# A two-layer encoder on one core: two pairs of heads in one score burst, the Exp table loaded early, one maximum per head, halves at the end, PSUM banks for turned blocks, and a new table of places

## The chip, the cores and the metric

The kernel runs on one core of one Trainium2 chip. The metric is device time in microseconds (us) of one execution. TensorE (PE; its weight loads are shown as PEld), VectorE (DVE), ScalarE (ACT), GpSimd (POOL) and SyncE (SP) each run their own instruction stream in order; DMA transfers are issued by SP, by POOL and, at the start, by ACT.

## The reference, cut to what matters

Two layers over 256 tokens of width 1024, everything in float32. A layer is an attention part with three groups of heads and a feed-forward part with a convolution:

```python
h = rms_norm(x, n1);  proj = h @ w_in            # 1024 -> 2560
# a: 4 heads, neighbourhood with a bias; d: 6 heads, dilated window; c: 6 query heads on 2 key heads
s = q @ k.T * scale (+ bias);  p = softmax(s);  out = p @ v
x = x + concat(rms_norm(out_a), rms_norm(out_d), rms_norm(out_c)) @ w_out
h = rms_norm(x, n2);  g, u = split(h @ w_gate_up)   # 1024 -> 2 x 2816
g = depthwise_conv_centred(g, cw, cb)               # 3 taps along the tokens
x = x + (gelu(g) * u) @ w_down
```

## The kernel before, in words

Tokens are two tiles of 128 partitions (t = 0, 1). Each product is made of three: a float32 operand is split into a rounded high part and a low rest, and `mm3` (line 695) multiplies high by high, high by low and low by high. A weight unit of up to 2048 columns comes by DMA into one of four `raw` buffers; ACT copies it to `hi` in chunks and DVE subtracts to make `lo` (`split`, line 666). `hi` and `lo` have two buffers each. During the feed-forward part of layer 0, six units of layer 1's output projection are split ahead and stored to DRAM (`keep`, line 624); layer 1 fetches them with DMAs that POOL issues into `hi` and `lo`.

**Start.** `load(0)` (line 640) issues the first loads by the list START: on ACT's queue the first two column blocks of x, on SP's queue the gains of the first norm (tile `gl0`, 8 KB), the identity, the four chunks of the first weight unit and the other six blocks of x, between each other. Then come the units 1 and 2 and the rest. x is turned block by block (`split_T`, line 708): two PE transposes (one for each t) give a block of 256 tokens; ACT scales it by its gain into `hT` (high), DVE makes the low part. Two blocks share one PSUM bank, and the planner below treats a bank as one thing. `warmed` (line 578) issues dummy bf16 matmuls, first 13, then 15 that fill gaps.

**Layers.** The projections (seven groups of columns, 12 units) accumulate in four PSUM banks (`psa`). The attention works in the other four banks (`psw`): for every pair of heads a burst of 12 score matmuls (`scores`, line 1210; two heads on the two halves of the rows, run side by side), then softmax (`softens`, line 1062: DVE's maximum, ACT's Exp with the sum, a reciprocal, a scaling), four transposes of the result (`turn`), and the product with the values (`weigh`). Projections and output projections are woven between. The heads of group c, which have no bias, take their maximum with one `reduce_max` for each t. The output projection of group a comes last (line 1305), each half of columns after the sums of squares of the group: `group_rstd` turns them (two transposes of `sqm`), DVE sums, POOL takes the root (`rstd`), and DVE adds to x (tile `xs`, named `const_x` in the profile). Then x is turned again for the second norm. The feed-forward part has 11 steps: gate (two PSUM tiles, the convolution on ACT and DVE, Gelu), up, and down, which accumulates four tiles of 128 x 512 (`dacc`). After the last step DVE adds each of the four to x, and in layer 1 SP stores each to the output (line 1443).

**What sets the order.** Everything is recorded first as a list of operations (`Plan`, line 238) and then put in order by a list scheduler (`order`, line 319): it takes the operation that could start first by its own table of costs (`cost`, line 473), and among those that could start at the same time the one of lowest rank. The rank is the place in the list, plus what `later` adds, plus an entry of the table PLACES (line 229) for this place. The tuple LANDS (line 52) gives the landing of each first load by its number in START; the landing of later DMAs is worked out from a rate. The engines then run their instructions in the order that came out, each waiting for its semaphores. SP's DMAs also wait in turn for eight semaphores, so the ninth DMA is issued only after the first has landed, and so on.

Of the kernel before, what the change touches and what calls it, by code (L numbers as in the profile page):

```python
# [11 lines left out]
F32 = mybir.dt.float32  # L12
# [38 lines left out]

LANDS = (4074, 3054, 5167, 3987, 5363, 6065, 7002, 7704, 8406, 9342, 10278, 10308, 10337)

# [171 lines left out]
def handover(a, b):  # L225
# [3 lines left out]
PLACES = {  # L229
# [5 lines left out]
}  # L235


class Plan:
    def __init__(self, tc):
        self.tc, self.ops, self.shift, self.burst, self.bursts, self.behind = tc, [], 0, None, {}, None  # L240
        for name, short in (("tensor", "PE"), ("scalar", "ACT"), ("vector", "DVE"), ("gpsimd", "POOL"), ("sync", "SP")):
            setattr(self, name, PlanEngine(self, short, getattr(tc.nc, name)))
# [26 lines left out]
    def add(self, engine, method, args, kw):  # L269
# [14 lines left out]
        if method == "matmul" and not kw["start"]:  # L284
            ins.append(args[0])
        o.ns, o.lat, o.size, o.kind = cost(engine.name, method, args, kw, ins)
        o.before, o.after, o.first, o.tiles = set(), [], [], []
        for v in ins + outs:
# [30 lines left out]
    def order(self):  # L319
# [79 lines left out]
        while len(done) < len(ops):  # L399
            best = None  # L400
            for e, r in ready.items():
                for i in r:
                    o = ops[i]
                    if e in opened:
                        if o.burst != opened[e]:
                            continue
                        at = at_of(o)
                    elif o.burst is not None:
                        at = at_of_burst(o.burst) if i == self.bursts[o.burst][0] else None
                    else:  # L410
                        at = at_of(o)
                    if at is not None and (best is None or (at, o.rank) < best[:2]):
                        best = (at, o.rank, i)
# [22 lines left out]
            if o.method == "dma_start":  # L436

                ring = e if i < self.first_loads else "SP"
                end = max(at + 1360, wires.get(ring, 0.0))
                shared = 0.0  # L440
                if i < self.first_loads:
                    shared = o.size if ring == "ACT" else min(o.size, 120 * max(0.0, wires.get("ACT", 0.0) - end))
                if e == "POOL":
                    end += 1000
                wires[ring] = end + shared / 120 + (o.size - shared) / (280 if i < self.first_loads else 335)
                end = wires[ring] + 1200
                if i < self.first_loads:
                    end = LANDS[sum(p.method == "dma_start" for p in ops[:i])]
# [24 lines left out]
def cost(engine, method, args, kw, ins):  # L473

    out = args[0]
    if method == "dma_start":
        w = out if isinstance(out, View) else args[1]
        small = min(out.shape[-1], args[1].shape[-1]) < 128
        spread = isinstance(args[1], bass.AP) and args[1].ap[0][0] == 0
        size = 4 * math.prod(w.shape) * (2 if small else 2 if spread else 1)  # L480
        return 620 if engine == "POOL" else 480, 0, size, None
# [33 lines left out]
def encoder_kernel(  # L515
# [73 lines left out]
    minus_half = const.tile([P, 32], F32, tag="mh", name="minus_half")  # L589
    nc.gpsimd.memset(minus_half, -0.5)  # L590


# [115 lines left out]
    def split_T(srcs, hi, lo, k0, g, name):  # L708
# [3 lines left out]
        for b in range(0, n, 2):  # L712
            m = min(2, n - b)
            ps = psw.tile([P, 2, S], F32, tag="w", name=f"pt_{name}_{b}")
            for i in range(m):
                k = b + i
                for t in range(NT):
                    nc.tensor.transpose(
                        ps[:, i, t * P : (t + 1) * P], srcs[t][:, k * P : (k + 1) * P], ident
                    )  # L720
            for i in range(m):
                k = b + i
                h, o = hi[:, k0 + k], lo[:, k0 + k]
                nc.scalar.activation(h, ps[:, i], AF.Copy, scale=g[:, k : k + 1])
                nc.vector.scalar_tensor_tensor(
                    o, ps[:, i], g[:, k : k + 1], h.bitcast(F32), ALU.mult, ALU.subtract
                )
# [147 lines left out]
    for l in range(DEPTH):  # L875
# [181 lines left out]
        class Head:  # L1057
# [3 lines left out]

            def softens(self, sps):

# [141 lines left out]
        def na_bias(h):  # L1205

            flat = nabs[l].rearrange("p r c -> p (r c)")
            return [flat[:, (h * RPB_ROWS + 3 - 2 * t) * GRID_W :][:, :S] for t in range(NT)]

        def scores(i):  # L1210

            two = heads[i : i + 2]
            sps = [psw.tile([P, NT, S], F32, tag="w", name=f"s_{z.name}") for z in two]
            g = two[0].group
            with nc.together():
                for t in range(NT):
                    for x, y in ((0, 0), (0, 1), (1, 0)):
                        for z, sp, rows_ in zip(two, sps, (LOW, HIGH)):
                            nc.tensor.matmul(
                                sp[:, t], turned[g + "q"][x][rows_, z.h // 2, t * P : (t + 1) * P],  # L1220
                                turned[g + "k"][y][rows_, z.kv if g == "c" else z.h // 2],
                                start=(x, y) == (0, 0), stop=(x, y) == (1, 0),
                            )
            for z, sp in zip(two, sps):
                z.softens([sp[:, t] for t in range(NT)])

# [146 lines left out]
        def gate(s):  # L1373
# [15 lines left out]
            nc.scalar.activation(B, A, AF.Gelu)  # L1389
            made[s] = B  # L1390

        def up(s):
# [9 lines left out]
        def down(steps):  # L1402
            ws = [unit() for _ in steps]
            for h in range(2):
                hs = slice(h * 512, (h + 1) * 512)
                for t in range(NT):
                    c = slice(t * P, (t + 1) * P)
                    for s, (wh, wl) in zip(steps, ws):
                        ch, cl = ready[s]
                        for j in range(2):  # L1410
                            mm3(
                                dacc[t][h], ch[:, j, c], cl[:, j, c], wh[:, j, hs], wl[:, j, hs],
                                s == 0 and j == 0, s == STEPS - 1 and j == 1,
                            )

# [21 lines left out]
        for h in range(2):  # L1437
            for t in range(NT):
# [3 lines left out]
                )  # L1442
                if l == DEPTH - 1:
                    nc.sync.dma_start(ov[:, t, hs], xs[:, t, hs])
    nc.emit()
# [69 lines left out]
```

## Time and profile before

| | us |
|---|---|
| median of 3 runs (614.57 to 614.73) | 614.73 |
| the profiled execution | 614.38 |
| its span, first to last instruction | 612.6 |
| PE busy in the span | 604.5 |
| DVE busy | 485.4 |
| ACT busy | 428.5 |
| POOL busy | 84.3 |

The difference of 1.8 us between the execution and its span lies ahead of the first and behind the last instruction. All of the kernel is emitted by one line (L470), so instructions are told apart by the tiles that they write and read: `psw_w<-const_ident,const_x` is a transpose of x, `psa_a<-wp_hi,act_hT` a projection, `psw_w<-act_ko,act_qo` a score matmul. The layers stand one after the other: attention of layer 0 up to about 113 us, its feed-forward part to about 308, attention of layer 1 to about 420, its feed-forward part to the end. A busy PE is not PE at its peak: a matmul's row lasts longer than the distance to the next matmul's start, so PE's pace is read from starts.

### The profile page before, as it was taken

The numbers are of one execution on the slowest core, as the hardware profiler recorded it, in microseconds if no ns is written. First come the engines' busy times: TensorE is split into PE (matmuls) and PEld (weight loads), VectorE is DVE, ScalarE is ACT, GpSimd is POOL, SyncE is SP. The second block draws the span as 40 slices with busy tenths as digits, with TensorE's granted clock in tenths as the row PEclk, the third lists the DMA queues.
The fourth block names the chain that finished last, engine by engine and source line by source line (L and its number), as shares of the span: only waits on it lengthen the run. The fifth ranks groups of instructions, "written<-read, shape, count | busy, mean of one in ns | idle before, by whom it ended". The sixth has DMA issues, their size and how long they took to land.

```text
span 612.6 us, 9883 instructions
## 1 busy us (share of the span) xinstructions
PE 604.5 (99%) x3484; PEld 525.2 (86%) x3484; DVE 485.4 (79%) x1000; ACT 428.5 (70%) x1064; POOL 84.3 (14%) x136
## 2 busy tenths in 40 slices
PE   8999999999999999999999999998999999999997
PEld 6998888888888888888899989887888888888885
DVE  4899989797788988887777788767877777777774
ACT  6789999696565766675588889857755656566661
POOL 2732130202400000000032214231000000000000
PEclk9999999999999999999999999999999999999999
DMA  8893403557589799987555626654665555556501
GB/s 272 294 294 141 139 25 105 184 159 242 166 225 326 247 360 326 349 293 251 155 155 182 215 70 240 206 178 129 202 217 179 175 197 201 167 185 205 189 18 68
DMA packets 85073, 121.44 MB, mean 198 GB/s; under 512 B 9864, under 2 KB 69608, under 8 KB 85024
## 3 DMA queue, kind: packets, MB, share of 16 engines
q1 hardware_dynamic: 82752, 112.17, 56.6%
q0 software_dynamic: 1728, 8.39, 4.0%
q8 instruction: 27, 0.44, 0.3%
q10 hardware_dynamic: 544, 0.26, 0.2%
q14 instruction: 22, 0.18, 0.1%
HBM read 110.93 MB, written 9.88 MB: 197 GB/s over the span
## 4 chain that ended last, share of the span: by engine, by line
PE 92%; DVE 2%; ACT 2%; POOL 1%; DMA 1%; issue 1%; SPq 0%; DVEq 0%; POOLq 0%
PE psw_w L470 51%; PE psa_a L470 41%; DMA const_x<-in_x_dram 1%; ACT act_s2k L470 1%; POOL small_rstd L470 1%; DVE const_x L470 1%; DVE wp_lo L470 1%; SPq L470 0%; DVE act_sw L470 0%; DVE act_z L470 0%; ACT wp_hi L470 0%; POOL small_ms L470 0%; ACT L470 0%; ACT act_z L470 0%; ACT act_hT L470 0%
## 5 line engine op out<-in xcount | busy, mean ns | idle before, releaser
L470 DVE TENSOR_TENSOR wp_lo<-wp_raw,wp_hi 128x512 fp32r<-128x512 f32 (+2 forms) x332 | 232.1, 735 | 53.9 <-ACT wp_hi L470 36.8
L470 ACT CAST wp_hi<-wp_raw 128x512 fp32r<-128x512 f32 (+2 forms) x332 | 202.5, 663 | 21.7 <-PE psa_a L470 9.1
L470 PE MATMUL psw_w<-act_hT,wp_hi 128*128 128x512 f32 x704 | 181.4, 393 | 0.0
L470 PEld LDWEIGHTS psw_w<-act_hT,wp_hi 128*128 128x128 f32 x704 | 128.1, 189 | 24.7
L470 PE MATMUL psa_a<-wp_hi,act_hT 128*128 128x384 f32 (+2 forms) x448 | 113.3, 332 | 0.5 <-ACT wp_hi L470 0.5
L470 PEld LDWEIGHTS psw_w<-act_hT,wp_lo 128*128 128x128 f32 x704 | 97.9, 190 | 6.9
L470 PE MATMUL psw_w<-act_hT,wp_lo 128*128 128x256 f32 x704 | 102.8, 282 | 0.0
L470 PEld LDWEIGHTS psa_a<-wp_hi,act_hT 128*128 128x128 f32 x448 | 78.1, 189 | 4.0 <-ACT wp_hi L470 0.8
L470 PE MATMUL psa_a<-wp_lo,act_hT 128*128 128x384 f32 (+2 forms) x224 | 74.2, 333 | 0.3 <-DVE wp_lo L470 0.2
L470 ACT COPY act_s2k<-psw_w 128x256 f32<-128x256 f32 x88 | 32.2, 371 | 58.7 <-PE psw_w L470 58.5
L470 PE MATMUL psa_a<-wp_lo,act_ch 128*128 128x512 f32 x176 | 69.4, 394 | 0.0
L470 PE MATMUL psa_a<-wp_hi,act_cl 128*128 128x512 f32 x176 | 69.4, 395 | 0.0
L470 PE MATMUL psa_a<-wp_hi,act_ch 128*128 128x512 f32 x176 | 68.9, 394 | 0.0
L470 DVE TENSOR_TENSOR act_s2k<-psw_w,act_s2k 128x256 f32<-128x256 f32 x88 | 36.7, 422 | 15.2 <-ACT act_s2k L470 14.9
L470 PEld LDWEIGHTS psa_a<-wp_lo,act_hT 128*128 128x128 f32 x224 | 42.2, 188 | 3.0 <-DVE wp_lo L470 1.7
L470 PEld LDWEIGHTS psa_a<-wp_hi,act_cl 128*128 128x128 f32 x176 | 33.2, 188 | 7.9 <-DVE act_cl L470 0.3
L470 PEld LDWEIGHTS psa_a<-wp_hi,act_ch 128*128 128x128 f32 x176 | 33.2, 189 | 6.7
L470 PEld LDWEIGHTS psa_a<-wp_lo,act_ch 128*128 128x128 f32 x176 | 33.1, 188 | 6.8
L470 DVE SCALAR_TENSOR_TENSOR act_s2k<-act_s2k,act_cw,act_s2k 128x255 f32<-128x255 f32 x88 | 36.8, 482 | 1.4 <-ACT act_s2k L470 1.3
L470 ACT ACTIVATE act_s2k<-act_s2k,act_cw 128x256 f32<-128x256 f32 x44 | 24.1, 595 | 18.0 <-DVE act_s2k L470 18.0
L470 ACT ACTIVATE act_s2k<-act_s2k 128x512 f32<-128x512 f32 x22 | 13.9, 631 | 30.0 <-DVE act_s2k L470 30.0
L470 POOL TENSOR_TENSOR small_rstd<-small_ms,const_mh 128x6 f32<-128x6 f32 (+2 forms) x26 | 31.7, 1218 | 2.2
(112 smaller groups left out, 794.7 us busy)
## 6 DMA issues: line engine op xcount, KB each, us to landing
wp_raw<-in_w_gate_up_dram SPq DMA_DIRECT2D x44, 1024.0 KB, 5.2
wp_raw<-in_w_down_dram SPq DMA_DIRECT2D x22, 1024.0 KB, 5.0
wp_raw<-in_w_in_dram SPq DMA_DIRECT2D x14, 768.0 KB, 6.3
wp_raw<-in_w_in_dram SPq DMA_DIRECT2D x8, 1024.0 KB, 8.8
wp_raw<-in_w_out_dram SPq DMA_DIRECT2D x8, 768.0 KB, 9.5
dram_khi<-act_mixT_hi SPq DMA_DIRECT2D x4, 768.0 KB, 9.5
dram_klo<-act_mixT_lo SPq DMA_DIRECT2D x4, 768.0 KB, 9.8
wp_lo<-dram_klo POOLq DMA_DIRECT2D x4, 768.0 KB, 5.4
```

The source lines that it names most:

```text
L470: getattr(o.engine.real, o.method)(*map(real, o.args), **{k: real(v) for k, v in o.kw.items()})
```

## The change

- `scores`: 16 bursts of one pair become 10. BURSTS says where two pairs (24 matmuls, four PSUM banks) go as one: heads d0 to d3, c0 to c3 and a0 to a3 in each layer.
- After the last Gelu of layer 0 ACT computes one Exp of a 128 x 1 constant, which loads the table of Exp there.
- `softens`: one `reduce_max` over both t for a head of group c.
- `split_T`: each turned block has a PSUM bank of its own.
- `down` of the last two steps in layer 1: the tile (t, h) = (1, 1) is computed as two tiles of 256 columns, the second in a bank of psw (`end`); DVE's addition and the store of this tile are split in the same way, 512 to 768 and 768 to 1024.
- The planner: other LANDS, other rates for DMAs (360 for 335 GB/s, 1000 for 1200 ns to land, no extra 1000 ns for POOL's), 1.5 times the size for stores to DRAM, 1290 ns for a change of table, ties broken by place; and a new PLACES with 69 entries for 49. Some stand at the first loads: 35 (`gl0`), 40 (x, blocks 2 and 3), and 89 to 91 (units 1 and 2).

```diff
-LANDS = (4074, 3054, 5167, 3987, 5363, 6065, 7002, 7704, 8406, 9342, 10278, 10308, 10337)
+LANDS = (4100, 3300, 5300, 3450, 5800, 6450, 7250, 8200, 8900, 9800, 10700, 10750, 10800)
 PLACES = {
-    715: 185, 722: 185, 772: -261, 980: -22, 982: -95, 983: -95, 1039: -192, 1146: -2, 1150: -159, 1350: 23,
+    35: 21, 40: 129, 59: -58, 60: -58, 61: -58, 75: -24, 89: -285, 90: -285, 91: -285, 497: 135, 499: 135, 500: 135,
...
+    3994: -106, 4040: 30, 4120: 17, 4169: -28, 4188: -44, 5572: 165,
 }
...
-                if e == "POOL":
-                    end += 1000
-                wires[ring] = end + shared / 120 + (o.size - shared) / (280 if i < self.first_loads else 335)
-                end = wires[ring] + 1200
+                wires[ring] = end + shared / 120 + (o.size - shared) / (280 if i < self.first_loads else 360)
+                end = wires[ring] + 1000
                 if i < self.first_loads:
                     end = LANDS[sum(p.method == "dma_start" for p in ops[:i])]
...
-            ps = psw.tile([P, 2, S], F32, tag="w", name=f"pt_{name}_{b}")
+            ps = [psw.tile([P, S], F32, tag="w", name=f"pt_{name}_{b + i}") for i in range(m)]
...
-                    for t in range(NT):
-                        nc.vector.reduce_max(nm[:, t : t + 1], sps[t], axis=AX.X, negate=True)
+                    nc.vector.reduce_max(nm, whole, axis=AX.X, negate=True)
...
+        BURSTS = {0: 2, 4: 1, 6: 2, 10: 1, 12: 2}
+        scored = {}
+
         def scores(i):
 
-            two = heads[i : i + 2]
-            sps = [psw.tile([P, NT, S], F32, tag="w", name=f"s_{z.name}") for z in two]
-            g = two[0].group
-            with nc.together():
-                for t in range(NT):
...
+            if i in BURSTS:
+                with nc.together():
+                    for n in range(i, i + 2 * BURSTS[i], 2):
+                        two = heads[n : n + 2]
+                        sps = [psw.tile([P, NT, S], F32, tag="w", name=f"s_{z.name}") for z in two]
+                        scored[n] = sps
...
             nc.scalar.activation(B, A, AF.Gelu)
             made[s] = B
+            if s == STEPS - 1 and l + 1 < DEPTH:
+                with nc.not_before("ACT"):
+                    nc.scalar.activation(few_out, minus_half[:, :1], AF.Exp)
...
+                    halved = l == DEPTH - 1 and steps[-1] == STEPS - 1 and (h, t) == (1, 1)
+                    if halved:
+                        end = psw.tile([P, S], F32, tag="w", name="end")
+                    for a, b in ((512, 768), (768, 1024)) if halved else ((hs.start, hs.stop),):
...
+        if l == DEPTH - 1:
+            hs = slice(768, 1024)
+            nc.vector.scalar_tensor_tensor(xs[:, 1, hs], hold["end"], r2[:, 1:2], xs[:, 1, hs], ALU.mult, ALU.add)
+            nc.sync.dma_start(ov[:, 1, hs], xs[:, 1, hs])
```

The first place where rows move is SP's queue at the start of the program; `act_s2k<-in_norm` is `gl0`, `wp_raw<-in_w_in` with 128x384 a chunk of the first unit, with 128x2x384 a half of unit 1, with 128x4x384 a whole unit (2, then 3). Before:

```order
L470 DMA act_s2k_81<-in_norm_g_dram 16x128
L470 DMA const_ident_89<-in_c_ident_dram 128x128
L470 DMA wp_raw_95<-in_w_in_dram 128x384 x2
L470 DMA const_x_79<-in_x_dram 128x2x256
L470 DMA wp_raw_95<-in_w_in_dram 128x384 x2
L470 DMA const_x_79<-in_x_dram 128x2x256 x2
L470 DMA act_s2k_131<-in_out_norm_g_dram 16x128
L470 DMA act_s2k_131<-in_norm_g_dram 16x128
L470 DMA wp_raw_141<-in_w_in_dram 128x2x384 x2
L470 DMA wp_raw_155<-in_w_in_dram 128x4x384
```

The same queue in the changed kernel, from its first DMA on:

```order
L473 DMA const_ident_81<-in_c_ident_dram 128x128
L473 DMA wp_raw_89<-in_w_in_dram 128x384
L473 DMA wp_raw_95<-in_w_in_dram 128x2x384 x2
L473 DMA wp_raw_105<-in_w_in_dram 128x4x384
L473 DMA wp_raw_89<-in_w_in_dram 128x384 x3
L473 DMA const_x_79<-in_x_dram 128x2x256 x2
L473 DMA act_s2k_129<-in_norm_g_dram 16x128
L473 DMA act_s2k_138<-in_out_norm_g_dram 16x128
L473 DMA act_s2k_138<-in_norm_g_dram 16x128
L473 DMA wp_raw_156<-in_w_in_dram 128x4x384
L473 DMA const_rot_163<-in_c_rot_dram 128x2x208
L473 DMA const_x_79<-in_x_dram 128x2x256
```

Units 1 and 2 moved ahead of three chunks of unit 0 and of all x on this queue; `gl0` went from first to behind them, and one load of x, which by its number is blocks 2 and 3, to behind unit 3 and `rot`.

The second place is PE at the end of layer 1's attention, where group a's output projection (`psa_a<-wp_..,act_mixT`), the transposes of `sqm` and those of x for the second norm meet. Before, from the transposes of `sqm` on:

```order
L470 MATMUL psw_w_162<-const_ident_89,act_sqm_1010 128x128 x2
L470 MATMUL psw_w_122<-const_ident_89,act_s2k_221 128x88
L470 MATMUL psa_a_153<-wp_hi_136,act_mixT_lo_886 128x512
L470 MATMUL psa_a_159<-wp_hi_136,act_mixT_hi_870 128x512
L470 MATMUL psa_a_159<-wp_lo_248,act_mixT_hi_870 128x512
L470 MATMUL psa_a_159<-wp_hi_136,act_mixT_lo_886 128x512
L470 MATMUL psw_w_120<-const_ident_89,const_x_79 128x128
```

In the changed kernel ten matmuls of the same unit stand behind the transposes of `sqm`, and these are the last rows of them and what follows; `wp_hi_167` and `wp_lo_180` are the parts of the next unit, the second half of columns:

```order
L473 MATMUL psa_a_169<-wp_hi_142,act_mixT_hi_889 128x512
L473 MATMUL psa_a_169<-wp_lo_151,act_mixT_hi_889 128x512
L473 MATMUL psa_a_169<-wp_hi_142,act_mixT_lo_904 128x512
L473 MATMUL psa_a_161<-wp_hi_142,act_mixT_lo_904 128x512
L473 MATMUL psa_a_297<-wp_hi_167,act_mixT_hi_889 128x512
L473 MATMUL psa_a_327<-wp_hi_167,act_mixT_hi_889 128x512
L473 MATMUL psw_w_133<-const_ident_81,const_x_79 128x128 x2
```

Four matmuls between the transposes of `sqm` and those of x became twelve, and two of the twelve read the next unit. That unit is fetched by POOL, whose queue is there, in the changed kernel:

```order
L473 TENSOR_TENSOR act_sqm_972<-act_sqm_972,act_sqm_893 128x256
L473 DMA wp_hi_167<-dram_khi_2861 128x1024
L473 DMA wp_lo_180<-dram_klo_2881 128x1024
L473 TENSOR_SCALAR small_ms_351<-small_ss_1412 128x2
L473 TENSOR_TENSOR small_rstd_357<-small_ms_351,const_mh_85 128x2
```

Before, the two DMAs of that unit stood ahead of the addition to `sqm`, with `wp_lo` first.

The third place is the end of PE's program in the changed kernel; `psw_w_83` is the tile `end`, `psa_a_169` the tile (t, h) = (0, 0) of the down product, and before the last rows were six of the tile (1, 1), 512 wide:

```order
L473 MATMUL psw_w_83<-wp_hi_142,act_ch_821 128x256
L473 MATMUL psw_w_83<-wp_lo_151,act_ch_821 128x256
L473 MATMUL psw_w_83<-wp_hi_142,act_cl_831 128x256
L473 MATMUL psa_a_169<-wp_lo_151,act_ch_821 128x512
L473 MATMUL psa_a_169<-wp_hi_142,act_cl_831 128x512
L473 MATMUL psa_a_169<-wp_hi_142,act_ch_821 128x512
L473 MATMUL psa_a_169<-wp_lo_151,act_ch_821 128x512
L473 MATMUL psa_a_169<-wp_hi_142,act_cl_831 128x512
```

The entry 5572 put the last five matmuls of tile (0, 0) behind the halves of tile (1, 1), so a tile of 512 columns is finished last again.

More of the change, by code (lines that the diff above doesn't have):

```diff
@@ L239, in __init__ @@
     def __init__(self, tc):
-        self.tc, self.ops, self.shift, self.burst, self.bursts, self.behind = tc, [], 0, None, {}, None
+        self.tc, self.ops, self.shift, self.burst, self.bursts, self.behind, self.table = tc, [], 0, None, {}, None, AF.Exp
         for name, short in (("tensor", "PE"), ("scalar", "ACT"), ("vector", "DVE"), ("gpsimd", "POOL"), ("sync", "SP")):
@@ L411, in order @@
                         at = at_of(o)
[L412 removed]
+                    if at is not None and (best is None or (at, o.rank, i) < best):
                         best = (at, o.rank, i)
@@ L479, in cost @@
         spread = isinstance(args[1], bass.AP) and args[1].ap[0][0] == 0
-        size = 4 * math.prod(w.shape) * (2 if small else 2 if spread else 1)
+        stored = isinstance(out, View) and out.tile.pool.dram
+        size = 4 * math.prod(w.shape) * (2 if small or spread else 1.5 if stored else 1)
         return 620 if engine == "POOL" else 480, 0, size, None
```

57 lines of the change are left out of this document (35 added, 22 removed), and 9 rows, old and new, of the table PLACES.

## The prediction

> **What bounds the kernel now.** I read the page first, for the busy shares, then PE's waits, then the start stretch by stretch, since that is where the change moves most. Page:
>
> ```profile
> PE 604.5 (99%) x3484; PEld 525.2 (86%) x3484; DVE 485.4 (79%) x1000; ACT 428.5 (70%) x1064; POOL 84.3 (14%) x136
> ```
>
> PE's waits (us in total, times, longest):
>
> ```profile
> PE psw_w L470 <- DVE const_x L470: 1.6, 2, 1.3
> PE psw_w L470 <- POOL const_warm L470: 1.0, 1, 1.0
> PE psw_w L470 <- ACT act_s2k L470: 0.5, 1, 0.5
> ```
>
> PE is busy 604.5 of 612.6 us, and its three largest waits together are 3.1 us. So the time is PE's program plus a few holes. Two things can move it: instructions that PE no longer spends (or spends anew), and holes that open or close. DVE and ACT count only where PE waits for them. There is little to win and any amount to lose.
>
> **The start: the largest term.** Windows of the first 20 us (the columns after the stretch are its length, busy time of PE, PEld, DVE, ACT and POOL, granted clock, DMA share and GB/s):
>
> ```profile
> 0.00:4.00 4.00, 3.02 (x15) 2.15 (x16) 0.00 (x0) 1.28 (x1) 2.73 (x10) 1.00 0.48 116
> 4.00:10.00 6.00, 5.95 (x35) 4.49 (x33) 3.44 (x8) 4.17 (x11) 0.00 (x0) 1.00 0.92 277
> 10.00:14.00 4.00, 3.50 (x23) 2.88 (x23) 2.56 (x8) 3.76 (x13) 0.34 (x2) 1.00 1.05 388
> 14.00:20.00 6.00, 6.00 (x33) 5.70 (x34) 4.32 (x9) 5.94 (x33) 2.82 (x5) 1.00 1.07 360
> ```
>
> The DMA engines are nearly full from 4 us on (share 0.92 and more), so a load arrives when the bytes issued ahead of it have gone. The DMA issues of the same stretch (KB each, median us from issue to landing):
>
> ```profile
> wp_raw<-in_w_in_dram SPq DMA_DIRECT2D x5, 768.0 KB, 9.2
> wp_raw<-in_w_in_dram SPq DMA_DIRECT2D x4, 192.0 KB, 4.1
> wp_raw<-in_w_in_dram SPq DMA_DIRECT2D x2, 384.0 KB, 6.0
> ```
>
> A load issued later waits longer than its own size explains: that is a queue served about in its order. The first loads that PE needs, on its timeline (start, us, instruction; in the last two rows ACT and DVE):
>
> ```profile
> 0.98 3.60 PE L470 MATMUL psw_w<-const_warm 128*128 128x256 bf16 x16 [0.98 <-POOL const_warm L470]
> 4.51 0.28 PE L470 MATMUL psw_w<-const_ident,act_s2k 16*128 16x16 f32 x1
> 6.72 0.44 PE L470 MATMUL psa_a<-wp_hi,act_hT 128*128 128x384 f32 x1
> 7.35 0.60 PE L470 MATMUL psw_w<-const_ident,const_x 128*128 128x128 f32 x4
> 8.61 0.47 ACT L470 ACTIVATE act_hT<-psw_w,const_gains 128x256 fp32r<-128x256 f32 x1
> 13.92 0.56 DVE L470 TENSOR_TENSOR wp_lo<-wp_raw,wp_hi 128x384 fp32r<-128x384 f32 x1
> ```
>
> Before, the gains (`gl0`, transposed at 4.51) are SP's first DMA and x's blocks 2 and 3 are transposed at 7.35. In the changed queue, as the change's rows show, units 1 and 2 (1536 KB) pass almost everything. The bytes ahead of `gl0` are then the identity, units 0 to 2, half of x: about 3.2 MB. Ahead of x's blocks 2 and 3, counting themselves and what ACT's queue carries, are 4392 KB = 4.50 MB: identity 64, units 0 to 3 3072, x 1024, `rot` 208, three gains 24.
>
> When that is moved: 116 GB/s × 4 us = 0.46 MB by 4.0. The rest, 4.04 MB: I take 3.02 MB of weights at some 370 GB/s (between the last two windows' 388 and 360), 8.2 us, and 1.02 MB of small-row loads at the second window's 277, 3.7 us. The last byte is moved at 4.0 + 11.9 = 15.9, and I add 1.3 us to land: the 384 KB half of unit 1, issued at about 6.0, landed at 11.9, when by the same sums its bytes would have been moved by 10.5. So blocks 2 and 3 land at **17.2** (15.8 with everything at 388 and no tail; 20 with everything at 277 and the tail). `gl0` by the same sum lands at about 13.3; PE would then wait there for some 8 us, since no product can start before the gains scale x, and after three matmuls again for x.
>
> From 17.2 on ACT sets the pace. The transposes of the first of these blocks take 0.35 us, and behind it on ACT stand 6 scalings into `hT`, 4 casts of weights and 3 squares before the last cast that this group of columns needs. Their pitches:
>
> ```profile
> 12.05 0.83 ACT L470 ACTIVATE act_hT<-psw_w,const_gains 128x256 fp32r<-128x256 f32 x2
> 12.76 0.64 ACT L470 ACTIVATE act_s2k<-const_x 128x512 f32<-128x512 f32 x1
> 13.38 3.49 ACT L470 CAST wp_hi<-wp_raw 128x384 fp32r<-128x384 f32 x8
> ```
>
> 0.36 (0.83 less the 0.47 of one), 0.62 (12.76 to 13.38) and 0.43 us (3.49 less one's 0.5, by 7): 2.2 + 1.9 + 1.7 = 5.8 us, so the last cast ends near 23.3; DVE's difference (0.56 us) ends near 23.9, and the nine matmuls that still need it, at 0.173 us each, end at **25.5**. The pitch is that of these two rows (14.54 to 18.29 for 22 matmuls before the second, 0.17 each):
>
> ```profile
> 14.54 0.45 PE L470 MATMUL psa_a<-wp_lo,act_hT 128*128 128x384 f32 x1
> 18.29 0.51 PE L470 MATMUL psa_a<-wp_hi,act_hT 128*128 128x384 f32 x2
> ```
>
> Before, the same point of the program, the end of the first group of columns, is at 14.54 + 22 × 0.173 = 18.4. Behind it PE has no hole of note either way. **Shift +7.1**; with the two ends of the landing, +5.7 to +9.9. I take +7.0.
>
> **Score bursts.** 16 become 10. One burst, between two transposes:
>
> ```profile
> 55.74 0.38 PE L470 MATMUL psw_w<-const_ident,act_z 128*128 128x128 f32 x2
> 56.05 0.97 PE L470 MATMUL psw_w<-act_ko,act_qo 64*128 64x256 f32 x12
> 56.94 0.33 PE L470 MATMUL psw_w<-const_ident,act_s2k 128*128 128x128 f32 x1
> ```
>
> From 55.74 to 56.94 are 1.20 us. Two transposes at 0.11 each (0.60 us for four, less the 0.27 of one, by 3) leave 0.98; twelve matmuls side by side as six at 0.115 are 0.69. So a burst costs about 0.30 us to enter and leave; six fewer are **−1.8** (−1.1 if 0.18 is saved). Against it stands that a burst of 24 takes four PSUM banks at once and waits until all are free. No row shows such a wait: it is between 0 and 0.5 us (the `act_s2k` wait above) for each of six, 0 to 3.0. I take 0, nearer to the rows, as PE's waits list no burst.
>
> **Exp table.** ACT loads it in the middle of layer 1's softmax, and PE waits behind it:
>
> ```profile
> 346.57 1.28 ACT L470 ACT_TABLE_LOAD   x1
> 350.45 0.33 PE L470 MATMUL psw_w<-const_ident,act_s2k 128*128 128x128 f32 x1 [0.50 <-ACT act_s2k L470]
> 300.50 0.62 ACT L470 CAST act_ch<-act_s2k 128x512 fp32r<-128x512 f32 x1 [2.06 <-DVE act_s2k L470]
> ```
>
> It moves to where ACT is idle for 2.06 us ahead of 300.50: the 1.28 us and a tiny Exp fit. **−0.5** (0 if another thing is late there). Without the cover it costs up to 1.3 at 300.
>
> **The second norm of layer 1.** Before, PE waits for DVE's sum into x, which waits for POOL's root:
>
> ```profile
> 417.30 0.71 POOL L470 TENSOR_TENSOR small_rstd<-small_ms,const_mh 128x2 f32<-128x2 f32 x1
> 418.04 1.41 DVE L470 SCALAR_TENSOR_TENSOR const_x<-psa_a,small_rstd,const_x 128x512 f32<-128x512 f32 x2 [0.96 <-POOL small_rstd L470]
> 418.85 0.44 PE L470 MATMUL psw_w<-const_ident,const_x 128*128 128x128 f32 x2 [1.33 <-DVE const_x L470]
> ```
>
> The 1.33 and a smaller wait behind it are the 1.6 us of `const_x` in PE's waits. Twelve matmuls of 0.23 (pitch below), 2.8 us, now lie in the chain's place, which would close them. But two of the twelve need the next unit's high part, which POOL fetches only when its buffer is free, about 3.1 us of PE work ahead. These fetches take:
>
> ```profile
> wp_lo<-dram_klo POOLq DMA_DIRECT2D x1, 512.0 KB, 3.8
> wp_hi<-dram_khi POOLq DMA_DIRECT2D x1, 512.0 KB, 4.6
> ```
>
> So PE waits 0.7 to 1.5 us for the fetch where it waited for DVE; with 0.85, **−0.7** (−1.5 to 0).
>
> **The tail.** PE's last pitch, and DVE's last addition:
>
> ```profile
> 607.97 0.40 PE L470 MATMUL psa_a<-wp_lo,act_ch 128*128 128x512 f32 x1
> 608.20 0.40 PE L470 MATMUL psa_a<-wp_hi,act_cl 128*128 128x512 f32 x1
> 608.64 0.75 DVE L470 SCALAR_TENSOR_TENSOR const_x<-psa_a,small_rx,const_x 128x512 f32<-128x512 f32 x1 [1.11 <-PE psa_a L470]
> 596.33 1.11 PE L470 MATMUL psw_w<-act_hT,wp_lo 128*128 128x256 f32 x8
> ```
>
> The halves were to make the last addition and the last store half as large. But in the changed order five matmuls of a 512 wide tile stand last, so the last addition is again 0.75 us and the last store 256 KB. Twelve matmuls of 0.231 (607.97 to 608.20) became 24 of 0.119 (1.11 less one's 0.28, by 7): 2.86 − 2.77 = **+0.1**. If the halves were really last, about −0.3.
>
> **No term.** One maximum over 512 elements in place of two of 256:
>
> ```profile
> L470 DVE TENSOR_REDUCE small_nm<-psw_w 128x1 f32<-128x256 f32 x12 | 4.4, 420 | 0.1
> L470 DVE TENSOR_REDUCE small_ss<-act_s2k 128x8 f32<-128x512 f32 x2 | 1.4, 683 | 0.3 <-ACT act_s2k L470 0.3
> ```
>
> 2 × 420 − 683 = 157 ns less on DVE for each of 12 heads, 1.9 us, on an engine that PE waits for only where shown above: 0, at best −0.5. The banks for turned blocks let ACT start a block earlier, which is already in the start's chain: 0. Other places of the table move work that has cover: 0, at worst +1.
>
> **Sum.** 614.38 + 7.0 − 1.8 − 0.5 − 0.7 + 0.1 = 618.5. The profiled execution is 0.35 under the median of the runs, so 618.8 for the median.
>
> **The rivals.**
> - *PE runs slowly after its wait.* At the start 16 dummy matmuls take 3.60 us (0.21 each, less the pipeline's end), and these five take 0.71:
>
> ```profile
> 5.99 0.71 PE L470 MATMUL psw_w<-const_warm 128*128 128x256 bf16 x5
> ```
>
> 0.71 less 0.27 for the end of one, by 4, is 0.11. So PE starts at half pace, though the granted clock reads 1.00 in the first window. If a wait of 8 us sends it back there, up to 3.4 us of work (the length of the slow start) takes twice as long, +1.7; part is hidden behind ACT, and I take +1.4: **620.2**. Chance 0.15. The Trainium skill ("TensorE: Matmul & The Clock Gate", Part 1: The HAM clock gate) says that after an idle window of some 3.4 us TensorE falls back to half clock and comes back after about as long of sustained work; by that rule this rival holds, and the slow first dummies agree with it (0.21 against 0.11 us), but no run here shows a fall back within a program.
> - *Bursts wait for four banks.* The 1.8 us are paid back: **620.5**. Chance 0.08. For it speaks that half of the banks of the attention hold results that ACT and DVE still read; against it, that PE's waits show nothing of the kind now.
> - *The start costs nothing (the other side).* If the queue isn't served in order, small loads pass large ones and `gl0` and x land about as before. Then 614.73 − 1.8 − 0.5 − 0.7 + 0.1 = **611.8**, faster. It decides at a loss of 1.7 us: x's blocks must land before some 10 us. For it speaks that no row shows a small load issued behind two megabytes; against it the 4.1, 6.0 and 9.2 us above. Chance 0.10.
> - *A start half as bad* (+3, if the queue is served in parallel by halves): **614.9**, chance 0.07.
>
> **How the numbers follow.** My case holds 0.60 (617.0 to 620.2). Range: from the partial start's upper side, 615.5, to 621.3, where a late landing (+9.7) with the other terms as taken stands; the faster rival, the half of the partial case and the far tail are left out, some 0.2. About 0.2%, 1.23 us, is what a measurement of this kernel tells from no change: faster than 613.5 0.10, within 0.07, slower than 616.0 0.83.
>
> **What would show it.** In the changed profile: the transposition of the gains near 13 us instead of 4.51, and x's `psw_w<-const_ident,const_x` for blocks 2 and 3 near 17; a wait of PE of about 8 us and a DMA named as its releaser; the first group of columns ending near 25.5; no wait before 350; PE's wait at the second norm of layer 1 on DMA into `wp_hi` instead of on `const_x`; the last addition on 128x512. I am wrong if the gains are turned before 9 us.

## The result, and the profile after

The changed kernel takes 619.74 us (median of 5 runs, 618.89 to 620.54) against 614.62 us (614.22 to 614.73): a ratio of 1.0082, 95% interval 1.0067 to 1.0097. It is 5.1 us slower; the forecast was 618.8 (615.5 to 621.3). The profiled execution took 620.54 us, the longest of the five, with a span of 618.8 us; the shortest, 618.89, had 617.1. Sizes read from the trace of the changed kernel carry that much play.

The page's first lines and PE's waits (us in total, times, longest):

```profile
PE 604.3 (98%) x3496; PEld 527.1 (85%) x3496; DVE 486.8 (79%) x989; ACT 428.0 (69%) x1065; POOL 85.7 (14%) x136
```

```profile
PE psw_w L473 <- DMA act_s2k<-in_norm_g_dram: 7.8, 1, 7.8
PE psa_a L473 <- DMA wp_hi<-dram_khi: 1.1, 2, 0.6
PE psw_w L473 <- POOL const_warm L473: 1.0, 1, 1.0
PE psw_w L473 <- DMA const_x<-in_x_dram: 0.2, 1, 0.2
```

PE's busy time is the same, 604.3 for 604.5 us. The span is 6.2 us longer, and one new wait, 7.8 us for the gains, is more than that. The two waits for `const_x` on DVE and the one for ACT's softmax (1.6 and 0.5 us before) are gone; 1.1 us for POOL's fetches of kept weights came in.

The windows of the start (length, PE, PEld, DVE, ACT, POOL, granted clock, DMA share, GB/s):

```profile
0.00:4.00 4.00, 3.02 (x15) 2.16 (x16) 0.00 (x0) 1.28 (x1) 2.73 (x10) 1.00 0.48 124
4.00:10.00 6.00, 1.23 (x9) 0.78 (x7) 0.00 (x0) 0.51 (x1) 0.00 (x0) 0.82 1.02 366
10.00:14.00 4.00, 1.00 (x5) 1.00 (x6) 0.65 (x2) 0.00 (x0) 0.00 (x0) 0.50 0.92 297
14.00:20.00 6.00, 5.77 (x30) 4.83 (x28) 3.62 (x8) 4.86 (x13) 0.00 (x0) 0.66 0.63 218
20.00:26.00 6.00, 6.00 (x39) 5.96 (x37) 4.78 (x11) 5.84 (x19) 1.70 (x4) 1.00 0.58 138
```

The DMA engines are as full as before (1.02 and 0.92), so nothing got slower there; they carry the weights of units 1 and 2 while PE, DVE and ACT stand. And the granted clock falls to 0.50. Three rows of PE's timeline set the end of the start:

```profile
13.00 0.25 PE L473 MATMUL psw_w<-const_ident,act_s2k 16*128 16x16 f32 x1 [7.77 <-DMA act_s2k<-in_norm_g_dram]
16.76 1.11 PE L473 MATMUL psw_w<-const_ident,const_x 128*128 128x128 f32 x4 [0.23 <-DMA const_x<-in_x_dram]
26.89 0.44 PE L473 MATMUL psa_a<-wp_hi,act_hT 128*128 128x384 f32 x1
```

The gains are turned at 13.00 (before 4.51), blocks 2 and 3 of x at 16.76 (before 7.35), and the second group of columns starts at 26.89 (before 18.46): **8.4 us later**. From there to the end the kernel wins 2.2 us back. In the table stand first starts in the two traces, and in that of the first two experiments:

| first start, us | before | changed | start alone | start put back |
|---|---|---|---|---|
| second group of columns | 18.46 | 26.89 | 26.41 | 18.74 |
| down product, layer 0 | 140.04 | 148.55 | 148.53 | 140.04 |
| second group of columns, layer 1 | 317.90 | 326.16 | 326.28 | 317.63 |
| down product, layer 1 | 440.92 | 447.09 | 449.21 | 437.89 |
| last matmul | 608.20 | 614.44 | 616.49 | 605.25 |

The loss is there by 27 us; what the change wins comes almost all between 318 and 441 us, in layer 1's attention.

### The profile page after: what moved, and what is told of

The parts are those of the page before. It is cut to its first block, busy times and chain, and to the rows that moved or that the text cites. A ratio compares the mean times of both kernels' runs of the same rounds, so it can differ in the third digit from the quotient of the medians.

```text
span 618.8 us, 9898 instructions
## 1 busy us (share of the span) xinstructions
PE 604.3 (98%) x3496; PEld 527.1 (85%) x3496; DVE 486.8 (79%) x989; ACT 428.0 (69%) x1065; POOL 85.7 (14%) x136
## 4 chain that ended last, share of the span: by engine, by line
PE 84%; DMA 4%; POOL 3%; DVE 3%; issue 3%; ACT 2%; SPq 1%; POOLq 0%
PE psw_w L473 48%; PE psa_a L473 36%; ACT act_s2k L473 2%; DMA wp_hi<-dram_khi 2%; DMA wp_raw<-in_w_in_dram 1%; POOL small_rstd L473 1%; DMA const_x<-in_x_dram 1%; DVE wp_lo L473 1%; SPq L473 1%; DVE act_cl L473 0%; ACT wp_hi L473 0%; POOL small_ms L473 0%; POOL act_sck L473 0%; POOL act_nab L473 0%; DVE act_z L473 0%
## 5 line engine op out<-in xcount | busy, mean ns | idle before, releaser
L473 PE MATMUL psa_a<-wp_hi,act_ch 128*128 128x512 f32 (+1 forms) x176 | 68.5, 392 | 0.0
```

Source lines behind the costliest of these rows:

```text
L473: getattr(o.engine.real, o.method)(*map(real, o.args), **{k: real(v) for k, v in o.kw.items()})
```

## The experiments

### The start undone, and the start alone

```diff
# start put back: the changed kernel
-    35: 21, 40: 129, 59: -58, ... 75: -24, 89: -285, 90: -285, 91: -285, 497: 135,
+    59: -58, ... 75: -24, 497: 135,
# start alone: the kernel before
 PLACES = {
+    35: 21, 40: 129, 89: -285, 90: -285, 91: -285,
```

> The changed kernel without the entries 35, 40 and 89 to 91: SP's first DMAs stand in the order of before. Theory (the start costs 8.4 us of PE's time, all else in the change gains about 2.2): PE's waits for the gains and for x are gone, PE's first projection starts near 6.7 instead of 15.2, and the time is 614.6 - 2.2 = 612.4 us (611.8 to 613.0). Rival (other places of the new table cost as well, and the start only half): 614 to 616 us.

> The kernel before with nothing but the five entries 35, 40 and 89 to 91 added. Theory (PE's own backlog of 45 matmuls behind the late x decides the end of the first group of columns, 8.4 us later than before): 614.6 + 8.4 = 623.0 us (622.0 to 623.8), with one wait of PE of 7 to 8 us for the gains and a granted clock of about 0.5 behind it. Rival (ACT's chain behind the late x decides, as the prediction had it, +7.0): 621.6 us.

Measured: 611.23 us with the start put back (ratio to before 0.9946, 0.9933 to 0.9960) and 622.83 with the start alone (1.0132, 1.0113 to 1.0151). The five entries cost 8.3 us on the old kernel and 8.5 on the new one, and the two changes add up: 8.26 − 3.34 = 4.92, measured 5.12. Without the entries the planner's order is another one only at the beginning: the last place at which PE's order differs is its 190th of 3496 instructions (with the start alone, the 208th of 3484). The shift with the start alone is 8.0 us at the second group of columns and between 8.3 and 8.5 in every later row of the table, so it is lost once and nothing later hides it. The rest of the change is worth 3.3 us, more than the 2.2 expected from the changed trace; 0.8 of the difference is that the profiled execution of the changed kernel took 0.8 us more than its median.

### Which late load is the price

Taking the entry of one late load away gives the planner another order, and it moved more than that:

```diff
# gains first
-    35: 21, 40: 129, 59: -58,
+    40: 129, 59: -58,
# x early
-    35: 21, 40: 129, 59: -58,
+    35: 21, 59: -58,
```

> The changed kernel without the entry 35 alone: the gains are SP's first DMA again, the two blocks of x stay late. Theory (x's landing near 16.6 us and PE's backlog behind it decide): PE starts near 6.7 us, does six matmuls instead of three, then waits some 8 us for x; three matmuls fewer behind x, 0.5 us: 619.2 us (618.6 to 619.8). Rival 1 (ACT decides behind x): 619.7. Rival 2 (the gains were the price): 612.5 to 615 us.

> The changed kernel without the entry 40 alone: the two blocks of x stand behind the second chunk of the first unit again, the gains stay behind units 1 and 2 and the rest of x and land near 13 us. Theory (PE's backlog decides): from 13.0 on PE has 48 matmuls of 0.173 and 16 transposes of 0.11 us, 10.1 us, 1.1 us until ACT has scaled the first block, and some 1.3 us for the half clock behind its wait: 25.5 instead of 26.9, 1.4 us less, 618.3 us (617.6 to 619.0). Rival (ACT's chain decides, 8.8 us from 13.5 and 1.5 us behind it): 2.5 us less, 617.2 us. Rival 2 (x was the price): 615 us or less.

Measured: 636.5 and 619.87 us. The first was far outside all three expectations, and for another reason than the landing of the gains. Its start ends 9.2 us late, 0.7 more than that of the changed kernel, but the down product of layer 0 starts 16.2 us later than there (164.77 for 148.55). So some 15.5 us are lost in layer 0's attention. The planner put the work of PE, ACT and DVE in another order up to about that point (PE's differs at 780 places, the last its 892nd of 3496; ACT's at 198), and PE waits. Of these waits the second and third lie in the start, the first and fourth in the attention; the two name 9.1 of the 15.5 us, and where the others are lost is not shown:

```profile
PE psw_w L473 <- ACT act_ch L473: 6.8, 3, 4.4
PE psw_w L473 <- DMA const_x<-in_x_dram: 4.6, 1, 4.6
PE psa_a L473 <- ACT wp_hi L473: 2.9, 1, 2.9
PE psw_w L473 <- ACT act_s2k L473: 2.3, 1, 2.3
```

So it says nothing on the time of a load. In the second the start ended 7.3 instead of 8.4 us late in the trace, since the gains landed at 13.5 and all of x was there, and the traced span is 1.4 us shorter (617.4 for 618.8). But the medians are the same (619.87 and 619.74), with spreads of 1.9 and 1.7 us, so the 1.4 us expected are neither shown nor refuted by the time. I then moved DMAs on SP's queue alone, behind the planner, with every engine's order kept:

```diff
-            for i in self.order():
+            turns = self.order()
+            for i, place in ((35, 0),):            # both loads: (40, 2), (35, 0)
+                turns.remove(i)
+                ahead = [j for j in turns if self.ops[j].engine.name == "SP"][place]
+                turns.insert(turns.index(ahead), i)
+            for i in turns:
```

> The changed kernel, every engine's order kept, with one move on SP's queue: the gains are issued first. Theory (the late x decides): the gains are turned near 4.5 us, PE does its three matmuls near 7 and then waits some 9 us for blocks 2 and 3 of x, which land near 16.6 as before; behind that nothing changes: 619.7 us (619.0 to 620.4). Rival (the 7.8 us wait for the gains is the price): 612 to 615 us.

> As the run before, and blocks 2 and 3 of x are issued behind the first chunk of unit 0 as well. Units 1 and 2 still stand ahead of the chunks 2 to 4 of unit 0 and of blocks 4 to 7 of x. Theory (whatever PE needs next decides by its landing): the second chunk lands near 11.0 us (2.56 MB ahead of it), is split by 12.0, and PE has 42 matmuls and 12 transposes left, 8.6 us, with about 1 us for a half clock: first group's end near 21.8 instead of 26.9, 3.4 us later than in the kernel before: 614.8 us (613.8 to 616.0). Rival (gains and x are the whole price): 611.3 us. Rival 2 (PE's backlog starts at the last x, near 13 us): 617 us.

Measured: 621.19 us with the gains first, 616.50 with the gains and x first. The first run's row of PE where x comes, and its windows:

```profile
16.59 1.11 PE L478 MATMUL psw_w<-const_ident,const_x 128*128 128x128 f32 x4 [8.71 <-DMA const_x<-in_x_dram]
```

```profile
10.00:14.00 4.00, 0.00 (x0) 0.00 (x0) 1.03 (x2) 0.92 (x2) 0.00 (x0) 0.65 0.96 319
14.00:20.00 6.00, 3.41 (x12) 3.41 (x13) 1.93 (x5) 3.28 (x9) 0.00 (x0) 0.50 0.63 212
20.00:26.00 6.00, 6.00 (x35) 5.87 (x35) 3.25 (x8) 4.38 (x12) 1.23 (x3) 0.88 0.43 131
```

The wait for the gains became one of 8.71 us for x, in the same place of the clock: x at 16.6 us is the price, and the gains are hidden in front of it. The time even rose by 1.4 us, and in the trace the second group of columns starts at 28.32 for 26.89. PE now starts its backlog at 16.59 from a standstill, and the half clock, which in the changed kernel had begun to run out on work ahead of x, stands behind it until about 21.4.

With both loads early 5.0 us of the 8.4 are still lost: PE waits 3.2 us for the cast of the second chunk of unit 0, which stands behind units 1 and 2:

```profile
11.93 0.69 PE L478 MATMUL psa_a<-wp_hi,act_hT 128*128 128x384 f32 x1 [3.18 <-ACT wp_hi L478]
```

That is the landing expected (split by 12.0); the sum was 1.7 us short (614.8 expected) because PE ran at half clock until 17.3: half of these 5.4 us, an estimated 2.7, is lost, where 1 us was expected. So the late loads stand in a row: the gains, the chunks of unit 0 and x are each late by themselves, and making one early uncovers the next.

### The half clock

```diff
-                getattr(o.engine.real, o.method)(...)
+                for _ in range(6 if o.method == "matmul" and i < 16 else 1):
+                    getattr(o.engine.real, o.method)(...)
```

> The changed kernel with 65 more dummy matmuls of 0.11 us ahead of the transposition of the gains (each of the first 13 is issued six times), so that PE is idle for less than 1 us before the gains land near 13.0. Theory (the half clock costs what stands behind x's landing: four transposes 0.77 for 0.44 and two matmuls 0.69 for 0.35 us): 0.65 us less, 619.1 us, and a granted clock of 1.00 throughout. Rival (the half clock costs 1.4): 618.3 us. Rival 2 (it costs nothing, x decides): 619.7 us.

Measured: 619.63 us (1.0093, 1.0069 to 1.0116). The clock stayed at 1.00 and x came at the same time:

```profile
10.00:14.00 4.00, 4.00 (x37) 3.44 (x36) 0.64 (x2) 0.28 (x1) 0.00 (x0) 1.00 0.95 304
14.00:20.00 6.00, 4.57 (x31) 3.87 (x29) 3.62 (x8) 4.68 (x14) 0.00 (x0) 1.00 0.63 213
```

```profile
16.66 0.66 PE L474 MATMUL psw_w<-const_ident,const_x 128*128 128x128 f32 x4 [1.26 <-DMA const_x<-in_x_dram]
```

In the trace the second group starts at 26.19 instead of 26.89, the 0.7 us expected. In the medians there are 0.1 us, less than either spread, so the time doesn't confirm it. What it does show is the backlog at full clock: from x's first transpose at 16.66 to 26.19 PE works without a pause, 9.5 us.

### The other parts, on the start of before

First the entry 5572 was taken out too, so that the halves stand last:

```diff
-    3994: -106, 4040: 30, 4120: 17, 4169: -28, 4188: -44, 5572: 165,
+    3994: -106, 4040: 30, 4120: 17, 4169: -28, 4188: -44,
```

> The first run's kernel (start as before) without the entry 5572 too, so that the last matmuls are those of the second half of tile (1, 1). The order of the end is the only difference to it. Theory: the last addition takes some 0.4 us instead of 0.75 and the last store is 128 KB: 611.2 - 0.3 = 610.9 us. Rival (the store of the other tiles, issued just ahead, decides): 611.2 us.

Measured: 610.55 us (610.45 to 610.68; 0.9931 of before, 0.9915 to 0.9947): 0.7 less than with the entry. The last rows of DVE, of the changed kernel and of this one:

```profile
614.88 0.75 DVE L473 SCALAR_TENSOR_TENSOR const_x<-psa_a,small_rx,const_x 128x512 f32<-128x512 f32 x1 [0.69 <-PE psa_a L473]
```

```profile
605.22 0.48 DVE L473 SCALAR_TENSOR_TENSOR const_x<-psw_w,small_rx,const_x 128x256 f32<-128x256 f32 x1 [0.55 <-PE psw_w L473]
```

It starts 0.32 us behind the last matmul (604.90) instead of 0.44, and takes 0.48 instead of 0.75. Against the run with the start put back the span is 0.9 us shorter, but 0.44 of that stands already at the down product of layer 1 (437.89 and 437.45) and isn't the tail's, whose own gain is the other 0.45. This version is the fastest of the study and beats both kernels. The rest goes from it: bursts cut in two, the Exp taken away, two maxima, a fetch in halves.

```diff
# bursts cut
+            cuts = {burst[12] for burst in self.bursts.values() if len(burst) == 24}
+            dummy = next(o for o in self.ops if o.method == "matmul")
...
+                if i in cuts:
+                    out = real(o.args[0]).rearrange("p (a b) -> p a b", b=P)
+                    o.engine.real.matmul(out, *map(real, dummy.args[1:]), start=True, stop=True)
# no Exp
+                if o.method == "activation" and o.args[0].shape == (P, 1) and o.args[2] == AF.Exp:
+                    args[2] = AF.Gelu
# two maxima
+                    for t in range(NT):
+                        run(args[0][:, t : t + 1], args[1][:, t], **o.kw)
# fetch in halves
+                if i == 4113:
+                    run(args[0][:, :512], args[1][:, :512])
+                    run(args[0][:, 512:], args[1][:, 512:])
```

> The kernel with the start of before and the halves last (610.55 us), each of its six bursts of 24 score matmuls cut in the middle by one dummy matmul; order and all else kept. Theory (a burst costs 0.28 us to enter and leave: 2 x 0.908 - 1.62 = 0.19 and 0.09 ahead of it): 6 x (0.28 + 0.11 for the dummy) = 2.3 us more, 612.9 us (612.5 to 613.2), of which 1.7 us are the bursts. Rival (the gain is hidden behind waits for PSUM banks or for ACT): 610.6 to 611.2 us.

> The same base with Gelu in place of the one Exp of the 128 x 1 constant, so that the table of Exp is loaded again at the first softmax of layer 1. Theory (PE waits there): 0.5 us more, 611.05 us (610.85 to 611.25), and a wait of PE of some 0.5 us on ACT at the first transposes of layer 1's softmax. Rival (the new order has cover there): 610.55 us.

> The same base with two maxima of 256 elements in place of one of 512 for each of 12 heads. Theory (DVE is off the path): 1.9 us more on DVE, nothing in the time: 610.55 us (610.3 to 610.8). Rival (the softmax of group c is on the path): 0.16 us for some of the heads, up to 611.5 us.

> The same base with POOL's fetch of the high part of the last unit of layer 1's output projection issued as two DMAs of 256 KB. The two matmuls that PE waits 0.8 us with read only the first half. Theory (the landing of that fetch is what PE waits for): the first half lands 0.3 to 0.7 us earlier: 610.1 us (609.9 to 610.4). Rival (both halves land together, or the second DMA holds POOL up and the root is late): 610.55 us or up to 611.0.

Measured, each against the 610.55: **612.12** (611.96 to 612.16), **611.60** (611.43 to 611.78), **611.17** (610.69 to 611.45) and **611.06** (610.59 to 612.54). The base ran on another occasion, where the kernel before took 614.46 against 614.53 here; a difference of 0.5 us is the least that I read as one, and each is read in the trace too.

*Bursts.* A burst of 24 in the changed kernel, and its two halves in the run with the cut:

```profile
54.70 1.70 PE L473 MATMUL psw_w<-act_ko,act_qo 64*128 64x256 f32 x24
```

```profile
45.98 0.98 PE L478 MATMUL psw_w<-act_ko,act_qo 64*128 64x256 f32 x12
47.11 0.98 PE L478 MATMUL psw_w<-act_ko,act_qo 64*128 64x256 f32 x12
```

From the burst's first start to the next instruction's are 1.63 us whole and 2.03 cut; 0.40, less 0.11 for the dummy, is 0.29 for a burst, against 0.30 predicted. But the time rose by 1.6 us and not by 2.4. In the trace the first cut's 0.4 us have shrunk to 0.2 by 54 us and the second, at 70, leaves no trace; the other four arrive at the end in full. So layer 0 hides two of its three.

*Exp.* The span rose by 1.0 us, twice what PE's wait before had shown, and no single wait of PE holds it. The load is in the middle of layer 1's attention again:

```profile
345.49 1.28 ACT L476 ACT_TABLE_LOAD   x1
```

Ahead of it PE is 0.14 us earlier than in the base, at 352 us 0.16 later, by 377 0.66 and by 398 0.98: pieces of 0.1 to 0.3 us, lost over 50 us.

*Two maxima.* In the trace 0.2 us, in small steps at group c's heads; the median says 0.6 with a spread of 0.8. Not nothing, but not settled between 0.2 and 0.6.

*Fetch in halves.* The base waits once; with the fetch split, PE's rows there are:

```profile
415.53 0.74 PE L473 MATMUL psa_a<-wp_hi,act_mixT_hi 128*128 128x512 f32 x2 [0.81 <-DMA wp_hi<-dram_khi]
```

```profile
415.04 0.72 PE L478 MATMUL psa_a<-wp_hi,act_mixT_hi 128*128 128x512 f32 x2 [0.17 <-DMA wp_hi<-dram_khi]
416.21 1.09 PE L478 MATMUL psw_w<-const_ident,const_x 128*128 128x128 f32 x8 [0.45 <-DVE const_x L478]
417.56 0.50 PE L478 MATMUL psa_a<-wp_lo,act_mixT_hi 128*128 128x512 f32 x1 [0.26 <-DMA wp_lo<-dram_klo]
```

The first half did come earlier, PE waits 0.17 us for it instead of 0.81, and PE stopped for the next two things instead: x's sum and the low part. POOL issued one DMA more, so its root starts at 413.65 (413.10 in the base). But that isn't what delays x's sum: DVE's additions wait for PE's own matmuls in both runs, first the base:

```profile
414.58 1.41 DVE L473 SCALAR_TENSOR_TENSOR const_x<-psa_a,small_rstd,const_x 128x512 f32<-128x512 f32 x2 [1.69 <-PE psa_a L473]
414.74 1.41 DVE L478 SCALAR_TENSOR_TENSOR const_x<-psa_a,small_rstd,const_x 128x512 f32<-128x512 f32 x2 [1.69 <-PE psa_a L478]
```

The sum comes as before, and PE is there sooner. What does come later is the low part, issued at 412.76 behind the second half (412.08 in the base). In the trace PE is 0.17 us behind the base ahead of this place and 0.48 behind it, so it is 0.3 us worse. The wait of 0.8 us is thus not the fetch's alone; x's sum and the low part end close behind it.

## Why the prediction was right, and where its sizes were off

| term | predicted | the runs |
|---|---|---|
| start | +7.0 | +8.3 (alone), +8.5 (undone) |
| bursts | −1.8 | about −1.2 (four of six × 0.29) |
| Exp | −0.5 | −1.0 |
| second norm of layer 1 | −0.7 | −0.8 to −1.0 (trace), less a new wait of 0.5 in the changed kernel |
| tail | +0.1 | 0.0 in the trace; −0.45 when the halves are last |
| one maximum | 0 | −0.2 to −0.6, not settled |

**The sum.** It gave +4.1, and +5.1 were measured. The start was 1.3 to 1.5 us too small and the bursts' gain 0.6 too large; the Exp, the norm and the maximum together gained some 1 us more than taken. That these errors partly cancel is luck. The direction isn't: it rests on the start, which outweighs all the rest. The PSUM banks of the turned blocks, the planner's rates and the other places of the table were not tested by themselves.

**The start, direction and cause.** Right, and shown from both sides: five entries of the table, 8.3 us. The queue served its loads in order: the gains were turned at 13.00 (13.3 predicted) after a wait of 7.8 us (some 8), and x at 16.76 (17.2), with a DMA as releaser each time.

**The start, its size.** The term was 1.4 us short, and the step that failed is "From 17.2 on ACT sets the pace", with nine matmuls behind DVE's last difference. x came 0.4 to 0.6 us earlier than that (16.76 here, 16.59 and 16.66 in two experiments) and the group still ended 1.2 us later. PE had done three matmuls before x came; the other 45 (0.173 each) and twelve transposes are 9.1 us of its own work, and it did them without a pause. With the clock at 1.00 that took 9.5 us (16.66 to 26.19), where the prediction had 8.3 (17.2 to 25.5). So the 1.4 us are 1.2 of backlog and 0.6 of half clock, less 0.4 for the earlier x. I had added up ACT's chain and never the backlog of PE, the engine that is busy 99% of the time. Two bounds of the working are off as well, without consequence: 4.04 MB at 388 GB/s end at 14.4, and at 15.8 only with the 1.3 us to land; and a late landing with the other terms as taken is 621.5.

**The half clock.** The rival gave a chance of 0.15 and a price of 1.4 us on top. Its mechanism came true: the fall is shown by the granted clock and by its cure with dummies. The measured 619.74 lies between the main sum's 618.8 and this rival's 620.2, so the time alone tells for neither. Its price depends on what stands behind the wait. Against 26.19, the start of the second group at full clock, it is 0.7 us in the trace of the changed kernel, where most of it ran out before x came, and 2.1 us (28.32) where x came first after the wait; where the chunk did, 2.7 us by the estimate above.

**Bursts.** The cost of one was right to 0.01 us; that all six reach the end was wrong, since layer 0 hides two. The feared wait for four banks appears in no list of PE's waits.

**Exp.** I priced the wait that the row named. The load costs as much again in pieces behind it, too small to be named in a list of waits.

**The second norm of layer 1.** As predicted, the wait moved from DVE's sum to POOL's fetch (0.58 us in the changed kernel and 0.8 with the start put back, against 0.85 predicted). Not predicted was the other 0.49 us of the 1.1, for the fetch of an earlier unit; the two rows of the changed kernel:

```profile
407.91 0.50 PE L473 MATMUL psa_a<-wp_hi,act_mixT_hi 128*128 128x512 f32 x1 [0.49 <-DMA wp_hi<-dram_khi]
424.93 0.74 PE L473 MATMUL psa_a<-wp_hi,act_mixT_hi 128*128 128x512 f32 x2 [0.58 <-DMA wp_hi<-dram_khi]
```

The first isn't there with the start put back. By both rows together PE waits 0.3 us more here than there, which is the smaller part of why the rest of the change is worth 3.3 us there and 2.2 in this trace.

**The tail.** Right: the last addition is 0.75 us on 512 columns as before, and without the entry 5572 the halves do gain, 0.45 us for the 0.3 priced.

**The other side** would have held if loads passed each other: it gave 611.8 us, and with the start undone the kernel takes 611.23. The queue's order is what decided it.

## What to carry to other kernels

When a load is moved back in a queue, work out its landing from the bytes ahead of it, and then add the whole backlog of the bound engine behind it, not only the longest chain of the helpers. Look for the next late load too: here three stood in a row, and making one or two of them early on the queue gained 3.2 us (619.74 to 616.50) or lost 1.4. A planner that takes landings from a fixed table doesn't see such a move, and taking one entry out of a table tuned as a whole can cost more (16.8 us here) than the entry did; move the one instruction behind the planner to test it.

## What the runs showed of the hardware

The granted clock of TensorE, us by us, in the changed kernel (PE's last work ahead of the wait ends at 5.2 us, and it starts again at 13.0):

```profile
7.00:8.00 1.00, 0.00 (x0) 0.00 (x0) 0.00 (x0) 0.00 (x0) 0.00 (x0) 0.93 1.06 392
8.00:9.00 1.00, 0.00 (x0) 0.00 (x0) 0.00 (x0) 0.00 (x0) 0.00 (x0) 0.50 1.07 398
17.00:18.00 1.00, 1.00 (x6) 1.00 (x6) 0.06 (x1) 1.00 (x4) 0.00 (x0) 0.50 0.82 273
18.00:19.00 1.00, 1.00 (x7) 1.00 (x7) 1.00 (x3) 1.00 (x4) 0.00 (x0) 0.95 0.09 26
```

It fell to a half 2.6 us into the wait and came back 5.1 us after work began again. Five experiments have such a fall too. All six in us, read from windows of 0.1 us ("entry" and "queue" say how the load was moved; the last column is the time from fall to return):

| | PE's work ends | clock falls | work begins | clock returns | time at half |
|---|---|---|---|---|---|
| changed kernel | 5.22 | 7.85 | 13.00 | 18.09 | 10.2 |
| start alone | 5.02 | 7.43 | 13.03 | 17.67 | 10.2 |
| gains first, entry | 8.22 | 10.38 | 16.73 | 20.62 | 10.2 |
| x early, entry | 6.45 | 9.70 | 13.54 | 16.52 | 6.8 |
| gains first, queue | 7.88 | 11.22 | 16.59 | 21.46 | 10.2 |
| both first, queue | 8.74 | 10.52 | 11.93 | 17.35 | 6.8 |

In the third PE also works for 1.0 us at 11.09. The falls come 1.8 to 3.3 us after the last work, the returns 3.0 to 5.4 us after work begins. Only the time at half is regular: 6.83 or 10.24 us, two or three times 3.41. That fits a clock that is set only at the edges of a window of 3.41 us, which runs on whatever the kernel does; it is an inference from these six rows. In the first 4 us the column reads 1.00 although the dummies run at half pace (16 in 3.60 us), so a start's half clock has to be read from the pitch of the matmuls.

The Trainium skill ("TensorE: Matmul & The Clock Gate", Part 1: The HAM clock gate) has the clock fall after an idle window of about 3.4 us, free-running, and come back after about 3.4 us of sustained work. The free-running window agrees with the times at half. The two thresholds don't: all six falls came before 3.4 us without work had passed, one of them in a pause of only 2.87 us (8.22 to 11.09), and four of the six returns took 4.6 to 5.4 us, with no pause of PE above 0.23 us in the work behind the wait.
